# Bulk loads of an infinity-norm kernel with a source of 16 x 8 rows, and its bulk results stored in six pieces

## The chip, the cores and the metric

The kernel runs on one core of a Trainium2 chip. The metric is the device time of one execution in microseconds; the runs of the kernel before took 626.88 and 626.92 us, median 626.9 us. A profile is taken of one execution, which has a time of its own.

## The reference

```python
def setup_inputs():
    rows = 8192
    cols = 8192
    return {"x": np.random.randn(rows, cols).astype(np.float32)}

def reference(x):
    return np.linalg.norm(x, ord=np.inf, axis=1)
```

For each of 8192 rows the largest absolute value of its 8192 floats: 268.4 MB are read and 32 KB written.

## The kernel before

A row of x is 32 KB. The 8192 rows are dealt out to 128 partitions, 64 rows to each: 48 in the bulk part and 16 in the tail (`n_tail`). A tile `t` holds two rows per partition (`B = 2`, so `W = 16384` floats, 64 KB), 8 MB in all, and there are three buffers for such tiles (`BUFS = 3`).

The bulk part (lines 300 to 307) is 24 tiles. The view `x_b` (line 274) splits the first 6144 rows into `A = 6` blocks of 1024 rows. In a block partition p owns eight consecutive rows of x, 256 KB, and the `G = 4` loads of the block take two of them each. So a load has 128 source rows of 64 KB, 256 KB apart, in one dimension, and 128 partitions as its destination. SP issues every load (line 303); VectorE reduces each landed tile with one `reduce_max` of absolute values (the helper `absmax`, line 296, is the line that all reduces carry) into two columns of `r_bulk`.

The tail (lines 309 to 320) is seven tiles whose loads are cut to the widths in `TAIL`, and each piece is reduced on its own into `part`. Here a partition owns 16 consecutive rows of x, so that source rows are 512 KB apart. The last tile (lines 327 to 358) is loaded in the twelve pieces of `LAST`; all but the last piece of each row leave their partial result beside the place where the last piece lands, so that a final reduce takes in both. After the first piece `part` is reduced into `r_tail`.

Two stores write the result: ScalarE's queue stores `r_bulk` (line 357) once the reduce of piece `len(LAST) - 3` is done, and SP's queue stores `r_tail` at the end (line 359).

What sets the order: SP issues the loads as the text has them, each waiting for the reduce that frees its buffer (the release of the tile three before) and, where the semaphore that it signals was used eight transfers earlier, for that transfer. VectorE takes the tiles in the same order. The functions that run when the program is finished move the first load to the start of SP's program (`start_first_load_early`), drop waits that others imply (`drop_implied_waits`), and let GpSimd wait for the last stores (`finish_on_pool`); the change leaves all of them as they are.

Of the kernel before, what the change touches and what calls it, by code (L numbers as in the profile page):

```python
# [3 lines left out]
logging.getLogger("concourse").setLevel(logging.ERROR)  # L4

# [1 line left out]

# [5 lines left out]
F32 = mybir.dt.float32  # L13
# [15 lines left out]
LAST = (  # L29
    [(0, w) for w in (2176, 1792, 1792, 1664)]  # L30
    + [(1, w) for w in (1664, 1408, 1280, 1152, 1024, 896)]
    + [(0, 768), (1, 768)]
)


HEAD, STEP = 32, 8


def segments(loads, cols):

    out, at = [], 0
    for i, w in enumerate(loads):
        end = at + w
        while at < end:
            r = at // cols
            to = min(end, (r + 1) * cols)
            out.append((i, r, at - r * cols, to - at))
            at = to
    return out
# [201 lines left out]
@with_exitstack  # L251
def kernel(
    ctx: ExitStack,
    tc: tile.TileContext,
    x: bass.AP,
    out: bass.AP,
    G: int = 4,
    B: int = 2,
    BUFS: int = 3,
    PAD: int = 256,  # L260
    LINE: int = 128,
):
    nc = tc.nc
    P = nc.NUM_PARTITIONS
    rows, cols = x.shape
    W = B * cols


    n_tail = B * (len(TAIL) + 1)
    n_bulk_rows = rows // P - n_tail  # L270
    assert n_bulk_rows % (G * B) == 0
    A = n_bulk_rows // (G * B)
    split = n_bulk_rows * P
    x_b = x[:split].rearrange("(a p n b) c -> a n p (b c)", p=P, a=A, n=G, b=B)
    out_b = out[:split].rearrange("(a p n b) -> p a (n b)", p=P, a=A, n=G, b=B)
    x_t = x[split:].rearrange("(p t b) c -> t p (b c)", p=P, b=B)
    out_t = out[split:].rearrange("(p t) -> p t", p=P)

    outp = ctx.enter_context(tc.tile_pool(name="outp", bufs=1))
    sbuf = ctx.enter_context(tc.tile_pool(name="sbuf", bufs=BUFS))  # L280

    segs = [segments(loads, cols) for loads in TAIL]
    k_max = max(sum(r == b for _, r, _, _ in s) for s in segs for b in range(B))
    parts_of = [sum(r == b for r, _ in LAST) - 1 for b in range(B)]
    assert sum(parts_of) <= PAD

    r_bulk = outp.tile([P, A, G * B], F32)
    r_tail = outp.tile([P, n_tail], F32)
    part = outp.tile([P, n_tail - B, k_max], F32)
    used = [HEAD, A * G * B, n_tail, (n_tail - B) * k_max]  # L290
    gap = -sum(-(-n // STEP) * STEP for n in used) % LINE
    outp.tile([P, gap], F32, name="gap")
    nc.gpsimd.memset(part[:], 0.0)  # L293

    def absmax(o, i):
        return nc.vector.reduce_max(  # L296
            out=o, in_=i, axis=X, apply_absolute_value=True
        )

    for a in range(A):  # L300
        for n in range(G):
            t = sbuf.tile([P, W + PAD], F32, tag="t")
            nc.sync.dma_start(out=t[:, :W], in_=x_b[a, n])
            absmax(
                r_bulk[:, a, n * B : (n + 1) * B],
                t[:, :W].rearrange("p (b c) -> p b c", b=B),
            )

    for i, loads in enumerate(TAIL):
        t = sbuf.tile([P, W + PAD], F32, tag="t")  # L310
        todo = segs[i]
        seen = [0] * B
        at = 0
        for j, w in enumerate(loads):
            nc.sync.dma_start(out=t[:, at : at + w], in_=x_t[i][:, at : at + w])
            at += w
            for _, b, c, n in [s for s in todo if s[0] == j]:
                k, lo = seen[b], b * cols + c
                absmax(part[:, i * B + b, k : k + 1], t[:, lo : lo + n])
                seen[b] += 1  # L320

    def after(ins, first, kind):
        info = mybir.DependencyInfo(kind, mybir.DependencyReason.SCHED_ONLY)
        tc.add_manual_dep(ins.ins, first.ins.name, info, reason="order")


    t = sbuf.tile([P, W + PAD], F32, tag="t")
    left = parts_of[:]
    col = [0] * B
    at, slot = 0, {}  # L330
    ends = [w for _, w in LAST[-B:]]
    lo = W - sum(ends)
    for b in range(B):
        slot[b] = -(-lo // LINE) * LINE + ends[b]
        lo = slot[b] + parts_of[b]
    assert lo <= W + PAD
    for j, (b, w) in enumerate(LAST):
        final = left[b] == 0
        to = slot[b] - w if final else at
        frm = b * cols + col[b]  # L340
        nc.sync.dma_start(out=t[:, to : to + w], in_=x_t[len(TAIL)][:, frm : frm + w])
        col[b] += w
        if final:
            r = n_tail - B + b
            absmax(r_tail[:, r : r + 1], t[:, to : slot[b] + parts_of[b]])
        else:
            left[b] -= 1
            k = slot[b] + left[b]
            done = absmax(t[:, k : k + 1], t[:, to : to + w])
            at += w  # L350
        if j == 0:

            ins = absmax(r_tail[:, : n_tail - B], part[:])
            after(ins, done, mybir.DependencyClass.NoSync)
        if j == len(LAST) - 3:

            ins = nc.scalar.dma_start(out=out_b, in_=r_bulk[:])
            after(ins, done, mybir.DependencyClass.Sync)
    nc.sync.dma_start(out=out_t, in_=r_tail[:])
    nc.at_finalize(clear_partials_early)  # L360
    nc.at_finalize(drop_implied_waits)
    nc.at_finalize(start_first_load_early)
    nc.at_finalize(finish_on_pool)
    nc.at_finalize(open_without_vector)
# [30 lines left out]
```

## Time and profile before

| | |
|---|---|
| median of the runs | 626.9 us (626.88 and 626.92) |
| time of the profiled execution | 626.5 us |
| its span, first to last instruction | 623.9 us |
| DMA, mean rate over the span | 430 GB/s |
| queue of SP's loads: packets, MB, share of 16 engines | 8064, 268.44, 99.7% |
| VectorE busy | 552.4 us (89%) |
| 24 bulk reduces, mean | 17.22 us |
| VectorE's wait for the 24 bulk loads | 70.5 us |

How to read it: the DMA share is the part of the span in which the 16 DMA engines had packets of the queue in hand. VectorE's wait is idle time just before its bulk reduces, put down to the load that ended it. The span is shorter than the time of the execution, which also has a start and an end outside the instructions.

### The profile page before, as it was taken

The numbers are of one execution on the slowest core, as the hardware profiler recorded it, in microseconds if no ns is written. First come the engines' busy times: TensorE is split into PE (matmuls) and PEld (weight loads), VectorE is DVE, ScalarE is ACT, GpSimd is POOL, SyncE is SP. The second block draws the span as 40 slices with busy tenths as digits, with TensorE's granted clock in tenths as the row PEclk, the third lists the DMA queues.
The fourth block names the chain that finished last, engine by engine and source line by source line (L and its number), as shares of the span: only waits on it lengthen the run. The fifth ranks groups of instructions, "written<-read, shape, count | busy, mean of one in ns | idle before, by whom it ended". The sixth has DMA issues, their size and how long they took to land.

```text
span 623.9 us, 151 instructions
## 1 busy us (share of the span) xinstructions
DVE 552.4 (89%) x63; POOL 0.3 (0%) x5
## 2 busy tenths in 40 slices
DVE  0588988889988899888898888988889999999999
POOL 0000000000000000000000000000000000000000
DMA  9999999999999999999999999999999999999998
GB/s 403 462 412 454 420 433 441 403 471 403 471 403 454 420 454 420 441 433 403 471 403 471 403 466 408 454 420 450 424 434 406 435 445 422 431 441 428 423 427 349
DMA packets 8849, 268.47 MB, mean 430 GB/s; under 512 B 1680, under 2 KB 1680, under 8 KB 3088
## 3 DMA queue, kind: packets, MB, share of 16 engines
q1 hardware_dynamic: 8064, 268.44, 99.7%
q10 hardware_dynamic: 784, 0.02, 0.1%
q14 instruction: 1, 0.01, 0.0%
HBM read 268.44 MB, written 0.03 MB: 430 GB/s over the span
## 4 chain that ended last, share of the span: by engine, by line
DMA 63%; DVE 36%; another core or an unknown queue 0%; DVEq 0%; issue 0%
DMA t<-in_x_dram 63%; DVE r_bulk L296 25%; DVE part L296 8%; DVE t L296 3%; DVEq L390 0%; DVE r_tail L296 0%
## 5 line engine op out<-in xcount | busy, mean ns | idle before, releaser
L296 DVE TENSOR_REDUCE r_bulk<-t 128x2 f32<-128x16384 f32 x24 | 413.3, 17220 | 70.5 <-DMA t<-in_x_dram 70.5
L296 DVE TENSOR_REDUCE part<-t 128x1 f32<-128x8192 f32 (+19 forms) x26 | 121.3, 4738 | 0.3
L296 DVE TENSOR_REDUCE t<-t 128x1 f32<-128x1792 f32 (+7 forms) x10 | 16.3, 1689 | 0.0
L296 DVE TENSOR_REDUCE r_tail<-t 128x1 f32<-128x772 f32 (+1 forms) x2 | 1.8, 947 | 0.0
L296 DVE TENSOR_REDUCE r_tail<-part 128x14 f32<-128x42 f32 x1 | 0.2, 185 | 0.0
L293 POOL MEMSET part<- 128x42 f32 x1 | 0.1, 133 | 0.0
L379 POOL MEMSET const-bfloat16-1.0<- 128x1 bf16 x1 | 0.1, 102 | 0.0
L379 POOL MEMSET const-uint8-127<- 128x1 uint8 x1 | 0.1, 102 | 0.0
L379 POOL MEMSET const-float32-0.0<- 128x1 f32 x1 | 0.1, 99 | 0.2 <-issue 0.2
L379 POOL MEMSET const-float32-1.0<- 128x1 f32 x1 | 0.1, 99 | 0.0
## 6 DMA issues: line engine op xcount, KB each, us to landing
t<-in_x_dram SPq DMA_DIRECT2D x2, 4672.0 KB, 37.5
t<-in_x_dram SPq DMA_DIRECT2D x2, 3520.0 KB, 36.2
t<-in_x_dram SPq DMA_DIRECT2D x1, 6336.0 KB, 36.4
t<-in_x_dram SPq DMA_DIRECT2D x1, 5696.0 KB, 40.5
t<-in_x_dram SPq DMA_DIRECT2D x2, 1792.0 KB, 34.3
t<-in_x_dram SPq DMA_DIRECT2D x1, 3392.0 KB, 37.6
t<-in_x_dram SPq DMA_DIRECT2D x1, 3008.0 KB, 44.2
t<-in_x_dram SPq DMA_DIRECT2D x1, 2496.0 KB, 27.3
```

The lines of the kernel that those rows point to most:

```text
L293: nc.gpsimd.memset(part[:], 0.0)
L296: return nc.vector.reduce_max(out=o, in_=i, axis=X, apply_absolute_value=True)
L379: nc = _bacc.Bacc("TRN2", target_bir_lowering=False, num_devices=1)
```

## The change

The bulk view gets another order. Instead of six blocks of 1024 rows there are `A = 3` blocks of 2048 rows (64 MB). A block is split first into 16 (`e`, `LANES`), each 4 MB; each of these into two halves (`h`) of 2 MB; each half into eight (`i`) of 256 KB; and these into the four loads' 64 KB. A load takes one 64 KB row for each of the 16 `e` and eight `i`, so that its source has dimensions 16 (4 MB apart), 8 (256 KB apart) and 16384 floats. The destination is the same tile with 128 partitions, in which partition `8 e + i` gets row (e, i). There are 24 loads of 8 MB as before, in the order of block, half, load.

The results of a block's half lie in eight columns of `r_bulk`; they are stored with one DMA for each block and half, six in all, and these wait for the reduce of piece `len(LAST) - 4` of the last tile, one piece earlier than the one store before.

```diff
+LANES = 16
...
+    H: int = 2,
...
-    assert n_bulk_rows % (G * B) == 0
-    A = n_bulk_rows // (G * B)
+    assert n_bulk_rows % (G * H * B) == 0
+    A = n_bulk_rows // (G * H * B)
     split = n_bulk_rows * P
-    x_b = x[:split].rearrange("(a p n b) c -> a n p (b c)", p=P, a=A, n=G, b=B)
-    out_b = out[:split].rearrange("(a p n b) -> p a (n b)", p=P, a=A, n=G, b=B)
+    dims = dict(a=A, e=LANES, h=H, n=G, b=B)
+    x_b = x[:split].rearrange("(a e h i n b) c -> a h n e i (b c)", **dims)
+    out_b = out[:split].rearrange("(a e h i m) -> a h e i m", a=A, e=LANES, h=H, m=G * B)
...
-    r_bulk = outp.tile([P, A, G * B], F32)
+    r_bulk = outp.tile([P, A, H, G * B], F32)
...
-    used = [HEAD, A * G * B, n_tail, (n_tail - B) * k_max]
+    used = [HEAD, n_bulk_rows, n_tail, (n_tail - B) * k_max]
...
-    for a in range(A):
-        for n in range(G):
-            t = sbuf.tile([P, W + PAD], F32, tag="t")
-            nc.sync.dma_start(out=t[:, :W], in_=x_b[a, n])
-            absmax(
-                r_bulk[:, a, n * B : (n + 1) * B],
-                t[:, :W].rearrange("p (b c) -> p b c", b=B),
-            )
+    for a, h, n in product(range(A), range(H), range(G)):
+        t = sbuf.tile([P, W + PAD], F32, tag="t")
+        nc.sync.dma_start(out=t[:, :W], in_=x_b[a, h, n])
+        absmax(
+            r_bulk[:, a, h, n * B : (n + 1) * B],
+            t[:, :W].rearrange("p (b c) -> p b c", b=B),
+        )
...
-        if j == len(LAST) - 3:
-
-            ins = nc.scalar.dma_start(out=out_b, in_=r_bulk[:])
-            after(ins, done, mybir.DependencyClass.Sync)
+        if j == len(LAST) - 4:
+
+            for a, h in product(range(A), range(H)):
+                ins = nc.scalar.dma_start(out=out_b[a, h], in_=r_bulk[:, a, h])
+                after(ins, done, mybir.DependencyClass.Sync)
```

More of the change, by code (lines that the diff above doesn't have):

```diff
@@ L6 @@
 from contextlib import ExitStack
+from itertools import product
 import concourse.bass as bass
```

## The prediction

> **What bounds the kernel now.** I read the page first: the busy times, the 40 slices and the DMA queues. It says that the transfers never pause while VectorE has room.
>
> ```profile
> span 623.9 us, 151 instructions
> ...
> DVE 552.4 (89%) x63; POOL 0.3 (0%) x5
> ...
> DMA  9999999999999999999999999999999999999998
> ...
> q1 hardware_dynamic: 8064, 268.44, 99.7%
> ```
>
> The queue that SP fills holds the 16 DMA engines for 99.7% of their span. Then I cut the span at the first and the last landing of a bulk load, with the busy times by window (columns: stretch, its length, VectorE, GpSimd, clock, DMA share, GB/s):
>
> ```profile
> 22.05:466.51 444.46, 396.05 (x23) 0.00 (x0) 1.00 1.00 434
> 466.51:582.74 116.23, 116.12 (x20) 0.00 (x0) 1.00 1.00 430
> ```
>
> 23 bulk loads land in 444.46 us: 19.32 us for 8.39 MB, 434 GB/s. Divided over 16 engines with 8 rows of 64 KB each, a row takes an engine 19.32 / 8 = 2.415 us, 27.1 GB/s. The timeline of VectorE shows how even this is, for a reduce starts when its load has landed:
>
> ```profile
> 22.05 17.22 DVE L296 TENSOR_REDUCE r_bulk<-t 128x2 f32<-128x16384 f32 x1 [22.05 <-DMA t<-in_x_dram]
> 41.35 17.22 DVE L296 TENSOR_REDUCE r_bulk<-t 128x2 f32<-128x16384 f32 x1 [2.08 <-DMA t<-in_x_dram]
> 60.68 17.22 DVE L296 TENSOR_REDUCE r_bulk<-t 128x2 f32<-128x16384 f32 x1 [2.11 <-DMA t<-in_x_dram]
> 80.09 17.22 DVE L296 TENSOR_REDUCE r_bulk<-t 128x2 f32<-128x16384 f32 x1 [2.19 <-DMA t<-in_x_dram]
> ```
>
> The starts are 19.30, 19.33 and 19.41 us apart: a pipe at a fixed rate, not a memory that answers now fast, now slowly. The waits complete the picture, VectorE's and then those of the SP queue:
>
> ```profile
> DVE r_bulk L296 <- DMA t<-in_x_dram: 70.5, 24, 22.1
> ```
>
> ```profile
> SPq L303 <- DVE r_bulk L296: 417.0, 21, 37.4
> ```
>
> VectorE waits 22.1 us for the first load and some 2.1 us for each other one. SP waits for a buffer, but with two loads queued behind the one whose buffer it waits for; that wait costs nothing. So the bulk stage costs 24 x 19.32 us, and what follows the last bulk landing is 623.9 - 466.5 = 157.4 us, in which VectorE works without a pause: 17.22 us for the last bulk tile and 139.6 us for the tail (121.3 + 16.3 + 1.8 + 0.2 in the groups).
>
> **The change, part by part.**
>
> *The addresses.* Bytes, row length (64 KB), number of loads (24), buffers and VectorE's reduces stay the same. What changes is that each load's source has an outermost dimension of 16 and 8 rows in each, where there was one dimension of 128 rows; the destination is still 128 partitions in order. All 56 loads of this trace have 128 rows in one dimension, so how the hardware deals a 16 x 8 source out to its engines is not to be seen here. The code says what it is meant to be: one block e for each engine, so eight neighbouring partitions. If that is already the deal, only addresses move. If it is not, the deal changes, and with it which engines write to which partitions at one moment.
>
> Lower end of its cost: nothing. If the fixed 2.415 us a row belongs to each engine, any deal of eight rows to each of 16 takes 19.32 us. A gain has a bound too: the first load lands at 22.05, 2.7 us later than 19.32, and the later ones deviate by under 0.1 us; more than 2 us is not there to be had. Upper end: if the fixed rate belongs to a group of partitions, and today's deal gives each engine a group of its own, then a deal that sends two engines into one group while another stands idle halves the rate: 2 x 19.32 = 38.64 us a load, and 24 x 19.32 = 463.7 us more in all. The two engines finish together and go on to the next group together, so nothing separates them again. Only their lead over each other is saved, and leads come from the start: the first load loses 2.7 us in all, so a lead is at most about one row. I assume that each engine's eight rows lie half in one group and half in another; then a lead of r rows makes four rows of both engines last 8 - r row times, where four would do unshared. With the slowest pair leading by a quarter of a row a load takes 2 x 7.75 x 2.415 = 37.4 us, with no lead 38.6; between the two I take 38.2 us. The addition is 24 x (38.2 - 19.32) = 453 us.
>
> Between ends so far apart the nearest row is the 2.415 us of a row itself. Its lack of any scatter says that a hard port, and not the memory, sets it; it does not say on which side the port lies. I take the upper end, as a judgement: a stage at a perfect rate can only lose by another deal, and this is the one thing that the edit alters in all 24 loads.
>
> The trace shows 434 GB/s for 128-partition loads and nothing of how partitions share a way in. [...]
>
> *The issue.* The SP issue of a bulk load took 327 to 719 ns (median 328). Two dimensions may cost the difference at most, 0.4 us; I take 0.1. Only the first one is on the path, the other 23 have about 20 us of queued loads as cover. Were that cover gone, 23 x 0.1 = 2.3 us.
>
> *Six stores instead of one, one reduce earlier.* The timeline of the end:
>
> ```profile
> 617.93 3.46 DVE L296 TENSOR_REDUCE t<-t 128x1 f32<-128x1152 f32 x3
> 621.32 1.81 DVE L296 TENSOR_REDUCE r_tail<-t 128x1 f32<-128x772 f32 x2
> 621.43 0.41 ACTq L357 DMA_DIRECT2D out_dram<-r_bulk  x1
> 623.15 0.35 SPq L359 DMA_DIRECT2D out_dram<-r_tail  x1
> ```
>
> The store now goes out at 621.43 with 0.41 us of issue and lands 2.5 us later, at 623.9; the tail store issues at 623.15 and lands 1.4 us later, at 624.55, so it ends last. The reduce before the 896-wide one ends about 1.0 us earlier, so six issues start at 620.4; at 0.41 to 0.47 us each they end by 623.2, and the last lands 1.4 to 2.5 us after its start, 624.2 to 625.3. Against 624.55 that is 0 to 0.75 us; ScalarE has nothing else queued. I take 0.2. [...]
>
> A further cost lies in semaphores: the loads of the last piece wait for the transfer that used the same semaphore eight transfers before (SP's waits show 38.9 us of this at L341, all with data still queued). If the six stores are counted in ahead of the last two loads, one of these waits for a store to land: 620.4 + 1.4, then about 2 us until its data is in, against a landing near 622.0 now: 1.5 to 3 us. In the program before, the store already stands ahead of the last two loads in the text, and yet the last of them issues at 611.2 us and the store at 621.43, so I take nothing and keep 3 for the range.
>
> *Sum.* The profiled execution took 626.5 us: span 623.9 and 2.6 around it; the median of the runs is 626.9, 0.4 above. Added: 453 + 0.1 + 0.2. In the profile 623.9 + 453.3 = 1077.2, in the runs 626.9 + 453.3 = 1080.
>
> **The rivals.**
>
> 1. *The deal doesn't matter: no change.* For it: the rate fits 16 equal engines exactly, and if the engines already take eight neighbouring partitions each, only addresses move. Tail rows lie 512 KB apart, so blocks of eight are 4 MB apart there as well, and the tail still moves 430 GB/s. Time: 626.9 + 0.1 + 0.2, 627; with a wait on a store's semaphore 630. It does not do what a new layout of addresses could be for, since no load shows a stall that 4 MB could take away. This is the case on the other side of 2%.
> 2. *Part of the price.* Either pairs drift apart until they no longer meet, or the addresses conflict in memory while the ways in do not. The measure of a disturbed load in this trace is the first one, 22.05 us: at 24 x 2.73 us more, 692. Pairs that drift apart half way through give 626.9 + 227 = 854. So 640 to 1000. Against it: equal sharing keeps a lead as it is, and the tail shows no address trouble.
> 3. *Faster by over 2%.* It needs 12.5 us, 0.5 us of each bulk load, 446 GB/s. Nothing in the even starts speaks for it.
>
> VectorE as the new bound is excluded: its 17.22 us a tile are unchanged, and under any of these cases a load takes longer.
>
> **How the numbers follow.** Full sharing 0.60, part of it 0.13, no change 0.25, faster 0.02. A change within 2% is about what a measurement of this kernel cannot tell from none; so faster 0.02, same 0.25, slower 0.73. The likeliest case has its own range: 626.9 + 24 x (37.4 - 19.32) = 1061 up to 626.9 + 463.7 + 4.5 = 1095. As the case of no change holds a quarter, the range must reach it: 626 to 1095, which leaves out what lies beyond either end.
>
> **What would show it.** Right: GB/s in the slices of the bulk stage near 217 to 220 and back above 400 in the tail; VectorE's starts 37 to 39 us apart with some 21 us idle before each; its wait for bulk loads up from 70.5 to over 500 us; the 157 us after the last bulk landing unchanged. Wrong: starts 19.3 us apart, which kills the shared way in; starts that go from about 38 towards 19 us within the stage (drifting pairs); a tail that slows down as well, or loads that differ among each other by block (addresses).

## The result, and the profile after

The changed kernel takes 1133.5 us (1132.97 and 1133.94) against 626.9 us: the ratio is 1.808, with a 95% interval of 1.800 to 1.816. The profiled execution of it has a span of 1131.1 us. The page shows where the time is, in the same lines that were read before:

```profile
span 1131.1 us, 156 instructions
...
DVE 552.4 (49%) x63; POOL 0.3 (0%) x5
...
DMA  9899998999999999999999999999999999899998
GB/s 222 185 222 211 197 222 185 222 211 197 222 188 220 211 197 222 190 218 211 197 222 190 218 213 195 222 192 216 213 195 222 192 216 216 327 436 434 428 431 363
...
q1 hardware_dynamic: 8208, 268.45, 99.7%
```

VectorE's work is the same to 0.1 us, the bytes are the same to 0.01 MB, and the 16 engines are as busy as before (99.7%). What fell is the rate: about 208 GB/s for the first 34 of 40 slices, 327 in the slice with the edge, and the old 430 after it. A row of nines for DMA is thus no sign of a full rate: an engine whose packets crawl is busy too. The packed trace holds the duration of every packet: of the 3072 rows of 64 KB that the bulk loads move, the median takes 2.42 us before and 5.10 us now. The windows from the first to the last bulk landing, and after it (stretch, length, VectorE, GpSimd, clock, DMA share, GB/s), put the edge between the bulk loads and the tail:

```profile
44.22:972.81 928.59, 396.05 (x23) 0.00 (x0) 1.00 1.00 208
972.81:1089.04 116.23, 116.23 (x20) 0.00 (x0) 1.00 1.00 432
```

23 bulk loads take 928.59 us, 40.37 us each instead of 19.32. VectorE's timeline has them at one beat, and its waits (total, times, longest) carry the difference:

```profile
44.22 17.22 DVE L300 TENSOR_REDUCE r_bulk<-t 128x2 f32<-128x16384 f32 x1 [44.22 <-DMA t<-in_x_dram]
84.60 17.22 DVE L300 TENSOR_REDUCE r_bulk<-t 128x2 f32<-128x16384 f32 x1 [23.16 <-DMA t<-in_x_dram]
124.98 17.22 DVE L300 TENSOR_REDUCE r_bulk<-t 128x2 f32<-128x16384 f32 x1 [23.16 <-DMA t<-in_x_dram]
```

```profile
DVE r_bulk L300 <- DMA t<-in_x_dram: 576.8, 24, 44.2
```

The account of the span: the first landing comes 22.2 us later (44.22 against 22.05), the other 23 loads cost 23 x (40.37 - 19.32) = 484.1 us, and what follows the last bulk landing has grown from 157.4 to 158.3 us. Together 507.2 us, which is 1131.1 - 623.9.

### The profile page after: what moved, and what is told of

The parts are those of the page before. It is cut to its first block, busy times and chain, and to the rows that moved or that the text cites. A ratio compares the mean times of both kernels' runs of the same rounds, so it can differ in the third digit from the quotient of the medians.

```text
span 1131.1 us, 156 instructions
## 1 busy us (share of the span) xinstructions
DVE 552.4 (49%) x63; POOL 0.3 (0%) x5
## 3 DMA queue, kind: packets, MB, share of 16 engines
q1 hardware_dynamic: 8208, 268.45, 99.7%
## 4 chain that ended last, share of the span: by engine, by line
another core or an unknown queue 47%; DVE 46%; DMA 7%; DVEq 0%; issue 0%
DVE r_bulk L300 37%; DVE part L300 8%; DMA t<-in_x_dram 7%; DVE t L300 1%; DVEq L394 0%; DVE r_tail L300 0%
```

## The experiments

The times given without an interval are of one execution each. Three theories could give the result; a "way" is a path that the first of them supposes, by which transfers enter a group of partitions of SBUF, the memory that holds the tiles. **A**: the 16 x 8 source gives each engine eight neighbouring partitions, and two engines then share one way into SBUF while another way stands idle. **B**: blocks 4 MB apart conflict in memory. **C**: a source with two dimensions of rows is slow as such.

**32 x 4 instead of 16 x 8.** The rows of a load are again neighbours in fours, 256 KB apart, and the 32 blocks are 4 MB apart in the first 128 MB and 2 MB in the other 64.

```diff
-    x_b = x[:split].rearrange("(a e h i n b) c -> a h n e i (b c)", **dims)
+    for nq in (4, 2):
+        r1 = r0 + nq * (split // (A * H))
+        xv = x[r0:r1].rearrange("(q h i n b) c -> h n q i (b c)", q=32, h=nq, n=G, b=B)
...
```

> The same kind of addresses as the change (neighbouring blocks 4 MB apart in two thirds of the bulk part and 2 MB apart in the rest, rows 256 KB apart), a source that again has two dimensions of rows, but 32 x 4 instead of 16 x 8. Theory A (two engines share a way into a group of partitions when each gets eight neighbouring ones): groups of four neighbours can be dealt so that each engine keeps to one group; bulk loads land 19.3 us apart, time 627 to 629 us. Theory B (the 4 MB spacing conflicts in memory): near 40 us a load in the first 16, over 950 us. Theory C (a source with two dimensions of rows is slow as such): 40.4 us a load, 1133 us.

Measured: 644.7 us, 1.030 times the kernel before (1.027 to 1.033). The loads run at the old beat of 19.3 us again from about the ninth on; the first ones are slow, 26.75 us to the first landing and then 23.3, 20.9, 21.5 and 19.8. C is refuted, and B as the cause of the doubling. But 18 us are lost, more than A expected; two runs below take that up.

**16 x 8 with the strides exchanged**: 16 blocks 256 KB apart, the eight rows 4 MB apart.

```diff
-    x_b = x[:split].rearrange("(a e h i n b) c -> a h n e i (b c)", **dims)
+    x_b = x[:split].rearrange("(a h i e n b) c -> a h n e i (b c)", **dims)
```

> The source stays 16 x 8, with the two strides exchanged: the 16 blocks are 256 KB apart and the eight rows of each 4 MB. Theory A: the destination is dealt as in the change, 40.4 us a load, 1133 us. Theory B: the engines are no longer 4 MB apart, so the loads speed up clearly, below 25 us, under 760 us. Theory C: 1133 us, as A.

Measured: 1133.9 us, as the change. The reduces of the middle of the stage start 40.4 us apart:

```profile
326.30 17.22 DVE L300 TENSOR_REDUCE r_bulk<-t 128x2 f32<-128x16384 f32 x1 [23.20 <-DMA t<-in_x_dram]
366.70 17.22 DVE L300 TENSOR_REDUCE r_bulk<-t 128x2 f32<-128x16384 f32 x1 [23.18 <-DMA t<-in_x_dram]
```

So the same form with other addresses gives the same price (1133.9 against 1133.5 us). It is the shape 16 x 8, not where its blocks lie.

**The kernel before, a tile in four loads of 32 partitions.** No address changes and the rows stay in one dimension; only how many partitions are written at a time does.

```diff
-            nc.sync.dma_start(out=t[:, :W], in_=x_b[a, n])
+            for p in range(0, P, 32):
+                nc.sync.dma_start(out=t[p : p + 32, :W], in_=x_b[a, n][p : p + 32])
```

> The kernel before with its addresses and one dimension of rows, but each bulk tile loaded by four DMAs of 32 partitions instead of one of 128. Theory A: 32 neighbouring partitions are half of the ways in, so two engines share each: 38.6 us (twice 19.32) to 40.4 us (as in the change) a tile, 1090 to 1133 us. Theories B and C: nothing that they name is in it, 19.3 to 20 us a tile, 627 to 645 us.

Measured: 1135.6 us, with 40.56 us a tile and 207 GB/s between the landings:

```profile
83.89:976.00 892.11, 378.85 (x23) 0.00 (x0) 1.00 1.00 207
```

That alone reproduces the loss in a kernel that has nothing of the change, and points to the side where partitions are written. That 32 partitions are half of the ways was a supposition of theory A; what is measured is the rate, 207 GB/s instead of 434.

**Only half of the blocks, and a lead made by hand.** In three runs only the first eight of the 16 blocks are loaded, so that a load is 4 MB and the DMA share is 0.50, as with eight of 16 engines at work. Between the first bulk load and the second, two of them have an extra load that is meant for engines 0–3 alone, into partitions that are otherwise free.

```diff
-        nc.sync.dma_start(out=t[:, :W], in_=x_b[a, h, n])
+        nc.sync.dma_start(out=t[:64, :W], in_=x_b[a, h, n][:8])
+        if (a, h, n) == (0, 0, 0):          # not in the first of the three runs
+            src = x[:128].rearrange("(e h i b) c -> h e i (b c)", e=4, h=4, b=B)
+            nc.sync.dma_start(out=t[64:80, :cols], in_=src[0, :, :, :cols])   # cols 8192, 16384
...
```

> The change with only the first eight of the 16 blocks loaded, reduced and stored: partitions 64-127 of the bulk part are left out, so a load is 4 MB on eight engines. If engines e and e + 4 share their ways in, the eight engines work at half rate as in the change: 40.4 us a load, 1133 us. If they would be limited by anything that all 16 engines share (memory, addresses in total), half the bytes take clearly less, 20 to 30 us a load.

Measured: 1101.8 us. For 12 loads the starts are 40.07 to 40.18 us apart, though half of the bytes are moved: eight engines show the loss (40.37 us with 16) without the other eight. From the 14th load on the beat shortens, 39.1, 38.4, 37.7, to 36.8 us. In the packet durations the shortest rows go from 4.2 us (between 157 and 315 us) to 3.0 us (between 630 and 787 us), as they would if leads grew slowly.

> The same half kernel (partitions 64-127 of the bulk part left out), with one load of 4 x 4 rows of 32 KB queued after the first bulk load, whose data nothing reads and which goes to partitions that nothing else writes. It keeps engines 0-3 for 4 x 1.21 us, a lead of two rows for engines 4-7. If pairs share fairly and keep a lead, a load takes 2 x (2 x 2.42 + 2 x 5.05) = 29.9 us from the second on and stays there to the end of the stage: 1133 - 23 x 10.5 + 10 = 900 us. If leads are lost, it goes back to 40.4: 1138 us.

Measured: 875.7 us. The beat is not the steady 29.9 expected: it goes 35.4, 36.1, 30.9, 29.4, 30.4, 34.2, 29.4, 27.4 and stays between 25.9 and 27.7 for 13 loads after these; the last two take 31.3 and 41.0. So by theory A a lead of two rows was worth more than its own two rows in the end; that it grew is the likely reading, and no run shows the lead itself.

> As the one before (partitions 64-127 of the bulk part left out), but with rows of 64 KB in the extra load: engines 0-3 are kept for 4 x 2.42 us, a lead of four rows. If pairs share fairly and keep a lead, the two of a pair never meet: 8 x 2.42 = 19.3 us a load from the second on, 1133 - 23 x 21.1 + 10 = 660 us, or up to 680 if memory loses some us as it did in the 32 x 4 run. If leads are lost: 1143 us.

Measured: 670.8 us. From the third load on the starts are 19.3 us apart:

```profile
43.71 17.21 DVE L300 TENSOR_REDUCE r_bulk<-t 64x2 f32<-64x16384 f32 x1 [43.71 <-DMA t<-in_x_dram]
73.20 17.21 DVE L300 TENSOR_REDUCE r_bulk<-t 64x2 f32<-64x16384 f32 x1 [12.28 <-DMA t<-in_x_dram]
92.72 17.21 DVE L300 TENSOR_REDUCE r_bulk<-t 64x2 f32<-64x16384 f32 x1 [2.31 <-DMA t<-in_x_dram]
112.00 17.21 DVE L300 TENSOR_REDUCE r_bulk<-t 64x2 f32<-64x16384 f32 x1 [2.08 <-DMA t<-in_x_dram]
```

This is the clearest sight of the cause. Apart from the one extra load, form, addresses, engines and bytes are those of the first of the three; engines 0–3 are merely meant to be four rows, some 9.7 us by the 2.42 us of a row, behind 4–7, so that by theory A the two of a pair are not in the same group of partitions, and the price of 21 us a load is gone. The packet durations say the same: between 92.72 and 459 us 97% of the rows take 2.42 us, as in the kernel before, and none over 2.61. The windows of the first and of this run, both with half of the engines busy, show 107 and 218 GB/s, 13.4 and 27.2 GB/s an engine:

```profile
43.70:485.36 441.66, 189.32 (x11) 0.00 (x0) 1.00 0.50 107
```

```profile
92.72:478.94 386.22, 344.22 (x20) 0.00 (x0) 1.00 0.50 218
```

**A lead for all 16 engines**, with three extra loads ahead of the change's own.

```diff
+    t = sbuf.tile([P, W + PAD], F32, tag="t")
+    for k, p in ((4, 0), (8, 32), (12, 64)):
+        src = x[: k * 16].rearrange("(e h i b) c -> h e i (b c)", e=k, h=2, b=B)
+        nc.sync.dma_start(out=t[p : p + 4 * k, :W], in_=src[0])
```

> The change with three extra loads ahead of the bulk part, of 4 x 4, 8 x 4 and 12 x 4 rows of 64 KB, whose data nothing reads. They are meant to give engines 0-3 twelve rows more, 4-7 eight and 8-11 four, so that engines e and e + 4 are four rows apart from the start. Theory A with fair sharing that keeps a lead: each pair then always works in different groups of partitions, bulk loads land 19.3 to 20.5 us apart after about 30 us, time 655 to 690 us. If leads are lost again, the starts go back to 40.4 us within the stage, 900 to 1160 us. Theories B and C: 40.4 us a load, 1133 + 30 = 1163 us.

Measured: 871.2 us, and neither of the two. The first landing came at 87.9 us, not at about 50, and then 20 loads took 26.0 to 26.8 us each, 316 GB/s:

```profile
114.00:642.70 528.70, 344.40 (x20) 0.00 (x0) 1.00 1.00 316
```

A beat that steady speaks for a lead that is kept. With rows of 2.42 us alone and 5.05 us shared (40.37 / 8), a lead of r rows makes, by theory A, 2 x (2.42 r + 5.05 (4 - r)), and 26.4 us would mean r = 2.7 for the slowest pair. This is a figure for the sum, not a lead that was seen: the rows of that stretch take from 2.42 to 4.74 us, and none the full 5.1. That the missing rows were lost because the extra loads met the bulk loads of other engines is likely from the late first landing, but no run shows it.

**How many share a way: eight loads of 16 partitions**, as the 32-partition run, with the kernel before's addresses. That four engines would share a way here is an estimate by theory A, from the doubled time with 32 partitions; no run shows the number.

```diff
-            nc.sync.dma_start(out=t[:, :W], in_=x_b[a, n])
+            for p in range(0, P, 16):
+                nc.sync.dma_start(out=t[p : p + 16, :W], in_=x_b[a, n][p : p + 16])
```

> The kernel before, with its addresses, each bulk tile loaded by eight DMAs of 16 partitions. [...] If sharing costs only the share: 4 x 19.32 = 77.3 us a tile, 626.5 + 24 x 58 = 2018 us. If each further engine adds to it (two take 40.4 instead of 38.6, 4.5% more), 79 to 85 us a tile, 2060 to 2200 us.

Measured: 1932.9 us, below both. The starts are 73.5 to 74.3 us apart (the last two 73.3 and 72.6), less than 4 x 19.32 = 77.3:

```profile
1112.46 17.22 DVE L296 TENSOR_REDUCE r_bulk<-t 128x2 f32<-128x16384 f32 x1 [56.33 <-DMA t<-in_x_dram]
1186.02 17.22 DVE L296 TENSOR_REDUCE r_bulk<-t 128x2 f32<-128x16384 f32 x1 [56.33 <-DMA t<-in_x_dram]
```

8.39 MB in 73.56 us are 114 GB/s, 28.5 GB/s for every four of the 16 engines. In loads of 128 partitions one engine brings 27.1, and in the change two bring 26.0 (8.39 MB in 40.37 us). Loads of 32 partitions have 1.8 times the rate of loads of 16 (207 against 114 GB/s). The 16 engines start a row spread over 1.9 us, out of 9.19 us that it takes, so the early ones can be at the next 16 partitions while the late ones are still at these; if those are other ways, this makes the 28.5 more than one way brings. How many share a way, and what four bring on one, is thus not shown.

**32 partitions, rows half as long**: the 32-partition loads, each cut into two of 32 KB rows.

```diff
-            nc.sync.dma_start(out=t[:, :W], in_=x_b[a, n])
+            for p, c in product(range(0, P, 32), range(0, W, W // 2)):
+                nc.sync.dma_start(
+                    out=t[p : p + 32, c : c + W // 2],
+                    in_=x_b[a, n][p : p + 32, c : c + W // 2],
+                )
```

> The run with loads of 32 partitions once more, each of them cut into two loads of 32 KB rows. It asks what the 5% are that two engines on one way cost beyond twice 19.32 us (40.55 us a tile there). If they are a lower rate of the way while two share it, the tile stays at 40.5 to 40.8 us and the time at 1135 to 1142 us. If they are a price for each row (0.24 us for two rows), twice as many rows add 16 x 0.12 = 1.9 us a tile: 42.4 us, 1180 us.

Measured: 1136.0 us and 40.56 us a tile. Twice as many rows cost nothing, so the 5% beyond twice 19.32 us are not a price per row; by theory A they are a lower rate while two share. Why two would lose stays open.

**The 18 us of the 32 x 4 run: its blocks all 2 MB apart, and its order exchanged.** These are two runs. The first has one view with 2 MB spacing in place of the change's; the second exchanges the order of the two spacings in the 32 x 4 run.

```diff
-    x_b = x[:split].rearrange("(a e h i n b) c -> a h n e i (b c)", **dims)
+    x_b = x[:split].rearrange("(a q h i n b) c -> a h n q i (b c)", q=32, **dims)   # all at 2 MB
...
-    for nq in (4, 2):
+    for nq in (2, 4):                       # order exchanged
```

> The 32 x 4 source with all blocks 2 MB apart, as they stand within the change's 64 MB. If the 18 us that the 32 x 4 run lost come from the 4 MB spacing, the first loads land 19.3 to 20 us apart and the time is 627.5 to 630 us: 626.5 + 0.4 for the first issue + 1.1 for the six stores. If they come from the 32 x 4 form, the first loads are as slow as there (26.8, 23.3, 20.9, 21.5 us) and the time is 640 to 647 us.

Measured: 628.7 us, 1.0032 times the kernel before (1.0020 to 1.0044), 19.30 to 19.46 us between the first starts. This run goes through the change's blocks of 64 MB, has two dimensions of rows as it has and the same six stores, and takes 32 groups of four rows where the change takes 16 groups of eight: 628.7 against 1133.5.

> The 32 x 4 run with its order exchanged: the eight loads with 2 MB spacing come first, the 16 with 4 MB after them. If the 4 MB spacing slows the loads whenever the engines run in step, loads 9 to 14 take 20 to 24 us each and the sum lost is again 12 to 18 us, 640 to 646 us. If only a cold start is slow, loads 9 to 24 take 19.3 us and the time is 628 to 633 us.

Measured: 640.4 us. The eight loads at 2 MB run at 19.3 us, and the first four at 4 MB take 22.6, 21.9, 21.3 and 21.2 us, though the engines have been at work for 158 us. So the slow loads come with the 4 MB spacing, not with the cold start. It wears off, as it did in the first run, within some five to eight loads.

**The six stores alone**, in the kernel before; the bulk results then go to the places of other rows.

```diff
+    out_b = out[:split].rearrange("(a e h i m) -> a h e i m", a=A // 2, e=16, h=2, m=G * B)
...
-        if j == len(LAST) - 3:
-            ins = nc.scalar.dma_start(out=out_b, in_=r_bulk[:])
+        if j == len(LAST) - 4:
+            for a, h in product(range(A // 2), range(2)):
+                ins = nc.scalar.dma_start(out=out_b[a, h], in_=r_bulk[:, 2 * a + h])
...
```

> The kernel before, with its loads, and the change's six stores in the change's place; the bulk results then land in the places of other rows, the work is the same. In the profile of the change the last of the six lands 1.06 us after the tail store, so 627.5 us against 626.5 (626.9 to 628.0). If the prediction's 0.2 was right, 626.7 us.

Measured: 627.8 against 626.6 us, a ratio of 1.0020 (1.0011 to 1.0029): 1.3 us. The end of its timeline:

```profile
620.47 3.98 ACTq L360 DMA_DIRECT2D out_dram<-r_bulk  x6
621.35 1.81 DVE L298 TENSOR_REDUCE r_tail<-t 128x1 f32<-128x772 f32 x2
623.19 0.35 SPq L362 DMA_DIRECT2D out_dram<-r_tail  x1
```

Six issues take 3.98 us, 0.66 us each, so the last of them ends 0.9 us after the tail store's issue, and its landing is now the last: in the profile of the change the six land 1.8 to 2.8 us after their issue, the tail store after 1.4.

## Why the prediction was right and wrong

**The sign was right, and the mechanism fits the runs.** The full sharing that had 0.60 fits what the runs show: the form of the source decides (628.7 us for 32 x 4 with the change's blocks, 1133.5 for 16 x 8), the price is on the side of the partitions (the kernel before with loads of 32 partitions: 1135.6), and it is gone when one extra load puts the engines out of step (the lead of four rows: 40.1 to 19.3 us a load). The trace does not name the engine of a packet, so the deal itself, eight neighbouring partitions to an engine, is inferred from these runs and not read off. So are the ways and the pairs, each of the first four engines with one of the next four: no run shows how many ways there are or which partitions belong to one. The halves of four rows were an assumption of the prediction; the packets of the change, whose pattern repeats after four rows, fit it, as told below.

**The size of one term was wrong, and with it the upper end of the range.** The prediction priced a load at 38.2 us, 453 us in all; measured are 506 us up to the last bulk landing. By the beat the missing 53 us are 24 x (40.37 - 38.2) = 52.1 us for the loads and 1.1 us of the first landing beyond them. The step that failed is the one that took the row's 2.415 us as the rate of the way, so that two engines would divide just that: 4.83 us a row, 38.64 us a load, as the most that sharing can cost. The row shows the rate of one engine, 27.1 GB/s; in the change two together have 26.0, which is not even one engine's. The packet durations show the slow row: two thirds of the bulk rows take 5.08 to 5.14 us, median 5.11, which is 24 x 8 x 0.28 = 54 us more than 4.83. The others, in order of their starts, are the first and the fifth row of a load and a third of the fourth and the eighth, the seams between groups of four, mostly 4.88 to 5.08 us. Because of them a load takes 40.4 us and not 8 x 5.11 = 40.9, about 0.5 us less. That is near the 0.44 us that the prediction gave to a lead of a quarter row; a small lead would make just such rows, but no run shows that it is one. With 1095 us the range stopped at a bound that was no bound. (Its 4.5 us for the rest are 0.4 + 0.75 + 3 = 4.15 by the terms named, which changes nothing.)

**"Equal sharing keeps a lead"** fits the full kernel, where the beat is the same from the first load to the last (40.15 to 40.41 us), and the run with three extra loads (26.0 to 26.8 us over 20 loads). It does not fit the half kernels with no lead and with two rows: the beat shortened, from 40.2 to 36.8 us and from 35.4 to 25.9, as it would with growing leads.

**The issue** of a bulk load was put at 0.1 us more. The view by line shows more than twice that, in the change and in the 32 x 4 run with 2 MB, where it was 328 ns before:

```profile
L306 SPq DMA_DIRECT2D t<-in_x_dram x24: 536/537/1346, 0.0 to 869.2; - x24
```

Only the first is on the path, as said. The first landing in the 2 MB run is at 22.8 us against 22.05; its longest issue is 769 ns against 719, so most of that delay has another cause, which no run shows. **The stores** were put at 0.2 us within 0 to 0.75; they cost 1.3. The step that failed took the issue from loads and stores with one dimension of rows (0.41 to 0.47 us), where the new form takes 0.61 and comes every 0.66 us. That the stores overlap, as its sum had it, was right: the six together cost 1.3 us, where six landings of 1.8 us or more, one after the other, would take over 10. **The wait on a store's semaphore** was rightly taken as nothing: SP's waits at the twelve last loads are 38.9 us in both profiles. The 2 us until a load's data is in, behind the 3 us of its range, were an estimate that no run shows.

**The rivals.** No change (0.25) needed the rate to be an engine's alone, or the deal to be the old one; the 32-partition run (1135.6 us) refutes the first, and the change beside the 32 x 4 run with 2 MB (1133.5 against 628.7) speaks against the second. Addresses, in the rival of a part price, are real but small: 4 MB apart costs 12 to 14 us over the first loads in the 32 x 4 form (16 loads took 320.8 us with the order exchanged, against 309.1 at 19.32; in the first 32 x 4 run the last bulk load landed at 481.5 us, against 467.3 with 2 MB). In the change nothing of it is to be seen, as 16 blocks 256 KB apart cost the same (1133.9 us). The argument that the tail's 512 KB rows speak against it was unsound: it took eight neighbours for an engine's share there too, and the full rate of the 128-row loads, 430 GB/s in the tail against 208 with 16 x 8, speaks against that.

## What to carry to other kernels

Here a load whose source reads as 16 blocks of eight rows took 40.37 us, and one of 128 rows, or of 32 blocks of four 2 MB apart, 19.3 us, though bytes, rows and engines are the same. When a 128-partition load has to run at the full rate, keep its source at 128 rows or, at a spacing of 2 MB as here, at 32 blocks of four, and check it by the beat of the landings, not by the DMA's busy share, which read 99.7% at half the rate. And a bound made by "two divide what one has" is an estimate of the limit, not the limit (38.64 us a load by it, 40.37 measured): leave room above it.

## What the runs showed of the hardware that was not expected

- Loads of fewer partitions had a lower rate: 207 GB/s with 32 partitions a load and 114 GB/s with 16, against 434 with 128, although the DMA share is 1.00 in all three.
- In the change two engines bring 26.0 GB/s together, less than one does in the kernel before (27.1); in the loads of 32 partitions it is 25.9, with 64 KB rows as with 32 KB rows (40.56 us a tile in both runs).
- The loss can go by a delay alone: one extra load of 16 rows, meant to hold four of eight engines for four rows, some 9.7 us, took a load from 40.1 to 19.3 us for the 21 loads from the third on; the last one of the stage, with the tail's loads behind it, took 30.5.
- In the 32 x 4 form source blocks 4 MB apart slowed the first loads to 21 to 23 us, and this wore off within five to eight loads; 2 MB apart they did not (19.30 to 19.46 us).
- The issue of a load whose rows have two dimensions took 536 ns instead of 328, a store's 610 instead of 347 to 406.
